# Down projection of a two-layer encoder: the seven block products in another order, one weight sum on VectorE instead of by an accumulating DMA, residual tiles in a tag of their own

## The chip, the cores and the metric

The kernel runs on one core of a Trainium2 chip. The metric is the device time of one execution in microseconds (us), given as the median over several runs. A profile is one execution of the same program, taken by the hardware profiler; its span starts with the first recorded instruction and ends with the last one.

## The reference

Two encoder layers work on a residual stream `x` of 1024 tokens by 1024 channels in float32. Each layer has an attention part (windowed in the first layer, a grid neighbourhood in the second, both with memory heads) and then a SwiGLU channel mixer. The change lies in the last matrix product of that mixer:

```
def reference(x, mem, ...):
    for i in range(DEPTH):                       # DEPTH = 2
        ...
        x = x + concat(y_tok, y_mem) @ w_out[i]
        h = rmsnorm(x, norm_ffn[i])
        gu = h @ w_gate_up[i]                    # (1024, 2 * 2816)
        x = x + (silu(gu[..., :D_FF]) * gu[..., D_FF:]) @ w_down[i]   # w_down[i]: (2816, 1024)
    return rmsnorm(x, norm_final)
```

## The kernel before, in words

**Arithmetic.** Activations lie with channels on the 128 partitions and tokens along the free side. Every float32 operand of a matmul is split into a high part (`hi`, line 106, a cast on ScalarE) and a low part (`lo`, line 109, a subtraction on VectorE). Each product is then three matmuls: high by high, high by low, low by high.

**The down projection** is done as a block product after Strassen and Winograd. The weight is cut into four blocks (even or odd 128-row blocks of the 2816 rows; first or second 512 columns), the activations into four as well, and seven products of block sums give what eight plain products would. The code numbers the products `i` = 0 to 6. The right sides (sums of activations) have been written to the DRAM tensors `b_d` by the gate-and-up stage (`hand_over`, lines 1001 to 1020). The left sides are made in place from the weight blocks by `left_side`:

- product 0 uses block `a` (even rows, first columns), which stays in SBUF in the first half of a tile `wd_kept`;
- product 1 uses the block of odd rows and first columns, loaded into a tile of the tag `raw`;
- product 3 uses `b`, the sum of the two blocks of the second columns; `b` is the second half of `wd_kept`;
- product 2 uses `b - a`, written over `a` (line 1083), so that it needs the sum that product 3 uses too;
- product 4 uses the first-column block minus the second-column block of the even rows. It is made while product 3 is prepared, over `b`, from two loads (lines 1099 to 1103);
- product 5 uses the odd first-column block minus the new `a` (line 1092), product 6 the odd second-column block.

The sum `b` is made by `first_sum` (lines 1057 to 1064): a plain load puts one block into `b`, and then a DMA that GpSimd issues on its own queue adds the other block onto it (`accum_op`, line 1062).

**Groups.** The 11 row blocks of a product are taken two at a time: `groups` has five of two and a last one of one. A full group is 24 matmuls (4 output tiles `m`, 2 row blocks, 3 terms), the last 12, a product 132. The main loop (lines 1218 to 1252) walks `dorder`, the pairs of product and group; at each step it calls `left_side` and `right_side` for the pair two places ahead. The split left sides `wd` rotate through 3 buffers (tag `whl`), the raw loads through 5 (tag `raw`), the `wd_kept` tiles are 6, and the right sides (`b_raw` from `b_d`, split into `hB`) share 16 buffers of the tag `h`.

**Results.** Products 0, 2 and 4 gather in four PSUM banks called `X`; products 1, 3 and 5 in four called `Y`; product 6 takes new `X` banks. A `start` flag clears a bank at products 0, 1, 3 and 6. After the last group of a product, `read` (lines 1144 to 1165) adds each bank on VectorE to the stream's tile `x` (line 1146). The residuals `xr` for this come back from DRAM by `residual` (lines 1121 to 1130), two tiles of the tag `raw` at a time.

**What sets the order.** The code does not fix the order in which an engine's instructions stand: a scheduler lays them out at build time, engine by engine, and may put an instruction far ahead of where the code calls it. Once laid out, each engine takes its queue strictly in order, and an instruction that waits holds up all that stand behind it. SyncE (SP) issues nearly all DMAs in the same way.

Of the kernel before, what the change touches and what calls it, by code (L numbers as in the profile page):

```python
# [9 lines left out]
F32 = mybir.dt.float32  # L10
# [7 lines left out]
P = 128  # L18
# [23 lines left out]
def trunk_kernel(ctx: ExitStack, tc: tile.TileContext, a: dict, out: bass.AP):  # L42
# [323 lines left out]
    for layer in range(2):  # L366
# [427 lines left out]
        with tc.tile_pool(name=f"fp{layer}", bufs=1, reuse_waits="tile") as fp:  # L794
# [259 lines left out]
                    kept[g] = fp.tile([P, 2, 2, HS], F32, tag="t8", name="wd_kept", bufs=6)[:, :n]  # L1054
                    rows(kept[g][:, :, 0], g, 0, slice(0, HS))

            def first_sum(g):

                p, n = groups[g]
                b, second_cols = kept[g][:, :, 1], slice(HS, D)  # L1060
                rows(b, g, 0, second_cols)
                nc.gpsimd.dma_start(
                    b, wd[p : p + n, 1].rearrange("n r c -> r n c")[:, :, second_cols], accum_op=ALU.add
                )

            def left_side(i, g):

                p, n = groups[g]
                first_cols, second_cols = slice(0, HS), slice(HS, D)

                def raw():
                    return raw_tile("wd_raw").rearrange("p (n c) -> p n c", c=HS)[:, :n]

                if i == 0:
                    keep_rows(g)
                a, b = kept[g][:, :, 0], kept[g][:, :, 1]
                if i == 0:
                    src = a
                elif i == 1:
                    src = raw()  # L1080
                    rows(src, g, 1, first_cols)
                elif i == 2:
                    nc.vector.tensor_tensor(a, b, a, op=ALU.subtract)
                    src = a
                elif i == 3:
                    src = b
                elif i == 4:
                    src = b
                elif i == 5:
                    src = raw()  # L1090
                    rows(src, g, 1, first_cols)
                    nc.vector.tensor_tensor(src, src, a, op=ALU.subtract)
                else:
                    src = raw()
                    rows(src, g, 1, second_cols)
                w = wp.tile([P, 2, D], F32R, tag="whl", name="wd", bufs=3)
                hi(two(w[:, 0], n), src)
                lo(two(w[:, 1], n), src, two(w[:, 0], n))
                if i == 3:
                    r = raw()  # L1100
                    rows(r, g, 0, first_cols)
                    rows(b, g, 0, second_cols)
                    nc.vector.tensor_tensor(b, r, b, op=ALU.subtract)
                for q in range(n):
                    left[i, p + q] = w[:, :, q * HS : (q + 1) * HS]

# [14 lines left out]
            def residual(i):  # L1121

                if i in (0, 2, 3, 4):
                    m0, f = {0: (0, 1), 2: (0, 0), 3: (4, 0), 4: (4, 1)}[i]
                    for m in range(m0, m0 + 4, 2):
                        t = raw_tile("xr").rearrange("p (n c) -> p n c", c=HS)
                        nc.sync.dma_start(
                            t, xr_d[layer][m : m + 2].rearrange("m p t -> p m t")[:, :, f * HS : (f + 1) * HS]
                        )
                        residuals[m, f], residuals[m + 1, f] = t[:, 0], t[:, 1]  # L1130
# [84 lines left out]
                if u.j == NF - 1 and n in (3, 4, 5):  # L1215
                    right_side(0, n - 3)
            norms = [Norm(), Norm() if is_a else Norm(HS, 7)]
            dorder = [(i, g) for i in range(7) for g in range(len(groups))]
            parts = iter(())
            hT = [[None] * NK, [None] * NK]  # L1220
            for at_, (i, g) in enumerate(dorder):
                if at_ + 2 < len(dorder):
                    left_side(*dorder[at_ + 2])
                    if at_ > 0:
                        right_side(*dorder[at_ + 2])
                if 1 <= at_ <= len(groups):
                    first_sum(at_ - 1)
                p, n = groups[g]
                if g == 0:
                    if i in (0, 6):  # L1230
# [115 lines left out]
```

## Time and profile before

| what | before |
|---|---|
| median of 3 runs | 2178.63 us (2178.58 to 2181.23) |
| the profiled execution | 2178.81 us |
| its span | 2176.9 us |
| busy share of the span: PE, DVE, ACT, POOL | 97%, 65%, 48%, 23% |
| mean granted TensorE clock | 0.989 |
| DMA moved | 287.22 MB, mean 132 GB/s |

PE is TensorE, DVE is VectorE, ACT is ScalarE, POOL is GpSimd. A row of a timeline gives start, duration, engine, line, operation, tiles and, in brackets, how long the engine sat idle before it and what ended that. Neighbouring instructions of the same kind are merged into one row with a count; PE's rows overlap a little, since matmuls are pipelined, so that the time of a block of matmuls is best taken from the start of one row to the start of the next. Line numbers are those of the kernel before.

### The profile page before, as it was taken

How to read it: one execution, taken by the hardware profiler on the slowest of the kernel's cores; microseconds unless marked ns; L12 is line 12 of the kernel's file. 1: busy time of each engine (PE TensorE's matmuls, PEld its weight loads, DVE VectorE, ACT ScalarE, POOL GpSimd, SP SyncE). 2: the span in 40 equal slices, each digit the busy share in tenths (PEclk: the TensorE clock that was granted, in tenths of full speed). 3: DMA queues.
4: the chain of work that ended last, by engine and by line, in shares of the span. 5: the costliest groups of instructions: out<-in, count | busy, mean ns of one | idle time of the engine just before them, and what ended most of it. 6: DMA issues, size and time to landing. Idle time of an engine off the chain costs nothing.

```text
span 2176.9 us, 28022 instructions
## 1 busy us (share of the span) xinstructions
PE 2120.3 (97%) x9946; PEld 1745.9 (80%) x9946; DVE 1408.2 (65%) x2302; ACT 1047.0 (48%) x1988; POOL 511.0 (23%) x557
## 2 busy tenths in 40 slices
PE   7999999999999999999999999999999999998997
PEld 6788888788888887788778888887888888887886
DVE  7676787775555555666766666667865455556575
ACT  6577785443333333434466566653433333343342
POOL 0344330223333321000233223203232233210000
PEclk9999999999999999999999999999999999999998
DMA  6321028333232238665232222274233232277652
GB/s 245 100 93 49 30 74 285 107 97 121 97 108 94 98 113 279 224 231 197 97 98 66 73 68 82 62 263 143 83 98 113 100 116 97 97 256 224 222 187 92
DMA packets 120076, 287.22 MB, mean 132 GB/s; under 512 B 12288, under 2 KB 18688, under 8 KB 119936
## 3 DMA queue, kind: packets, MB, share of 16 engines
q1 hardware_dynamic: 109888, 266.81, 37.0%
q10 hardware_dynamic: 7040, 12.85, 1.6%
q0 software_dynamic: 3008, 5.77, 1.5%
q8 instruction: 79, 1.29, 0.2%
q14 instruction: 61, 0.50, 0.1%
HBM read 210.40 MB, written 68.94 MB: 128 GB/s over the span
## 4 chain that ended last, share of the span: by engine, by line
PE 73%; issue 14%; DVE 4%; DMA 3%; ACT 3%; POOL 1%; SPq 0%; DVEq 0%; POOLq 0%; ACTq 0%
PE X L879 21%; PE Y L879 16%; PE mm L139 13%; PE X L1178 5%; PE Y L1178 4%; PE po L139 4%; PE S L559 3%; PE O L622 3%; PE pT L602 2%; DMA b_raw<-b_d 1%; ACT p L574 1%; DMA wd_kept<-in_w_dn 1%; DVE pl L109 1%; DMA wm_raw<-in_w_mem 1%; PE bc L242 0%
## 5 line engine op out<-in xcount | busy, mean ns | idle before, releaser
L879 PE MATMUL X<-hT,wgu 128*128 128x512 f32 x1056 | 259.1, 395 | 0.6 <-ACT g L896 0.6
L879 PE MATMUL Y<-hB,wgu 128*128 128x512 f32 x1056 | 255.5, 391 | 0.0
L1178 PE MATMUL X<-hB,wd 128*128 128x512 f32 x1056 | 246.4, 394 | 7.9 <-DVE wd L109 7.9
L879 PE MATMUL X<-hB,wgu 128*128 128x512 f32 x1056 | 247.8, 390 | 0.0
L1178 PEld LDWEIGHTS X<-hB,wd 128*128 128x128 f32 x1056 | 200.4, 190 | 51.4 <-DVE wd L109 8.7
L879 PEld LDWEIGHTS X<-hT,wgu 128*128 128x128 f32 x1056 | 198.2, 188 | 48.2 <-ACT g L896 1.0
L879 PEld LDWEIGHTS Y<-hB,wgu 128*128 128x128 f32 x1056 | 198.2, 188 | 43.4 <-issue 1.0
L879 PEld LDWEIGHTS X<-hB,wgu 128*128 128x128 f32 x1056 | 198.3, 188 | 41.8
L106 ACT CAST wgu<-wS 128x1024 fp32r<-128x1024 f32 x88 | 92.5, 1051 | 257.8 <-POOL wS L838 157.1
L587 POOL TENSOR_SCALAR p<-p,stat 128x384 f32<-128x384 f32 (+1 forms) x256 | 140.8, 569 | 313.3 <-DVE stat L584 203.7
L109 DVE TENSOR_TENSOR wgu<-wgu_raw,wgu 128x1024 fp32r<-128x1024 f32 (+1 forms) x88 | 84.8, 964 | 189.5 <-ACT wgu L106 189.5
L139 PE MATMUL mm<-hT,wqk 128*128 128x512 f32 x672 | 199.9, 405 | 0.1
L1178 PE MATMUL Y<-hB,wd 128*128 128x512 f32 x792 | 184.8, 395 | 7.1 <-DVE wd L109 7.1
L139 PE MATMUL po<-yT,wo 128*128 128x512 f32 x768 | 184.8, 394 | 0.0
L1178 PEld LDWEIGHTS Y<-hB,wd 128*128 128x128 f32 x792 | 151.3, 191 | 39.7 <-DVE wd L109 7.9
L106 ACT CAST hB<-b_raw 128x512 fp32r<-128x512 f32 x154 | 90.3, 618 | 163.9 <-DMA b_raw<-b_d 156.8
L139 PEld LDWEIGHTS po<-yT,wo 128*128 128x128 f32 x768 | 142.4, 188 | 29.6 <-issue 1.0
L838 POOL TENSOR_TENSOR wS<-wgu_raw 128x512 f32<-128x512 f32 x44 | 73.6, 1672 | 378.9 <-DVE wgu L109 378.9
L109 DVE TENSOR_TENSOR wgu<-wS,wgu 128x1024 fp32r<-128x1024 f32 x88 | 110.4, 1254 | 62.5 <-ACT wgu L106 62.5
L574 ACT ACTIVATE p<-p,stat 128x256 f32<-128x256 f32 (+1 forms) x192 | 112.3, 586 | 52.0 <-DVE stat L570 49.4
L109 DVE TENSOR_TENSOR hB<-b_raw,hB 128x512 fp32r<-128x512 f32 x154 | 100.8, 689 | 53.1 <-ACT hB L106 52.8
L109 DVE TENSOR_TENSOR pl<-pT,ph 128x384 fp32r<-128x384 f32 (+1 forms) x256 | 118.8, 494 | 21.0 <-ACT ph L106 17.9
(161 smaller groups left out, 3782.6 us busy)
## 6 DMA issues: line engine op xcount, KB each, us to landing
wgu_raw<-in_w_gu SPq DMA_DIRECT2D x92, 512.0 KB
b_raw<-b_d SPq DMA_DIRECT2D x70, 512.0 KB
b_d<-c SPq DMA_DIRECT2D x88, 256.0 KB
wd_raw<-in_w_dn SPq DMA_DIRECT2D x40, 512.0 KB
b_d<-t SPq DMA_DIRECT2D x66, 256.0 KB
wo_raw<-in_w_out SPq DMA_DIRECT2D x32, 512.0 KB
wd_kept<-in_w_dn SPq DMA_DIRECT2D x30, 512.0 KB
x<-in_x SPq DMA_DIRECT2D x32, 256.0 KB
```

The lines of the kernel that those rows point to most:

```text
L106: nc.scalar.copy(dst, src)
L109: (eng or nc.vector).tensor_tensor(dst, src, h.bitcast(F32), op=ALU.subtract)
L139: nc.tensor.matmul(ps[:, :n], l, r, start=start and i == 0 and j == 0, stop=stop and i == len(order) - 1 and j == 2,)
L559: nc.tensor.matmul(s_[:, :n], Q[self.h][:, qb * P : (qb + 1) * P], k, start=j == 0, stop=j == 1)
L574: nc.scalar.activation(p[:, :n], p[:, :n], AF.Exp, bias=m1, scale=-1.0, accum_out=s1)
L587: nc.gpsimd.tensor_scalar(p[:, :n], p[:, :n], ri[:, i : i + 1], 1.0, op0=ALU.mult, op1=ALU.mult)
L602: nc.tensor.transpose(tr[:, j * P : (j + 1) * P], p[:, j * P : (j + 1) * P], ident)
L622: nc.tensor.matmul(o[:, c0 : c0 + w * P], self.value(j), t[:, s0 : s0 + w].rearrange("p j q -> p (j q)"), start=j == js[0] and t is self.p ...
L838: sub = lambda o, p_, q_: nc.gpsimd.tensor_tensor(o, p_, q_, op=ALU.subtract)
L879: nc.tensor.matmul(ps, l, r, start=n in (0, 1, 3, 6) and k == 0 and i == 0, stop=k == 3 and i == 2, skip_group_check=True,)
L1178: nc.tensor.matmul(bank, l, r, start=i in (0, 1, 3, 6) and p == 0 and n == 0, stop=p == HF - 1 and n == 2, skip_group_check=True,)
```

## The change

The products are now walked in the order 0, 1, 3, 2, 4, 5, 6. `first_sum` and its accumulating DMAs are gone: at product 3 two raw tiles are loaded on SP's queue and added on VectorE into `b`. Product 2 still takes `b - a`, and now comes after product 3. The difference for product 4 is made at product 4 from two raw tiles. The residuals take tiles of the tag `S` (2 buffers, which the gate-and-up stage uses before) in place of tiles of the tag `raw`.

```
-            def first_sum(g):
-                p, n = groups[g]
-                b, second_cols = kept[g][:, :, 1], slice(HS, D)
-                rows(b, g, 0, second_cols)
-                nc.gpsimd.dma_start(
-                    b, wd[p : p + n, 1].rearrange("n r c -> r n c")[:, :, second_cols], accum_op=ALU.add
-                )
...
                 elif i == 3:
+                    r, o = raw(), raw()
+                    rows(r, g, 0, second_cols)
+                    rows(o, g, 1, second_cols)
+                    nc.vector.tensor_tensor(b, r, o, op=ALU.add)
                     src = b
                 elif i == 4:
-                    src = b
+                    src, o = raw(), raw()
+                    rows(src, g, 0, first_cols)
+                    rows(o, g, 0, second_cols)
+                    nc.vector.tensor_tensor(src, src, o, op=ALU.subtract)
...
-                if i == 3:
-                    r = raw()
-                    rows(r, g, 0, first_cols)
-                    rows(b, g, 0, second_cols)
-                    nc.vector.tensor_tensor(b, r, b, op=ALU.subtract)
...
-                        t = raw_tile("xr").rearrange("p (n c) -> p n c", c=HS)
+                        t = fp.tile([P, 2, HS], F32, tag="S", name="xr", bufs=2)
...
-            dorder = [(i, g) for i in range(7) for g in range(len(groups))]
+            dorder = [(i, g) for i in (0, 1, 3, 2, 4, 5, 6) for g in range(len(groups))]
...
-                if 1 <= at_ <= len(groups):
-                    first_sum(at_ - 1)
```

**Order, first place: VectorE's queue at the end of product 0 in the first layer, before.** `wd_kept_7395`, `7412`, `7440`, `7535`, `7574` and `7613` are the kept tiles of groups 0 to 5; `wd_7615` is the left side of the last group of product 0, and `wd_7655` that of the first group of product 1.

```order
L109 TENSOR_TENSOR hB_7620<-b_raw_7618,hB_7620 128x512
L1083 TENSOR_TENSOR wd_kept_7412<-wd_kept_7412 128x2x512
L1083 TENSOR_TENSOR wd_kept_7440<-wd_kept_7440 128x2x512
L109 TENSOR_TENSOR wd_7615<-wd_kept_7613,wd_7615 128x512
L109 TENSOR_TENSOR hB_7660<-b_raw_7658,hB_7660 128x512
L109 TENSOR_TENSOR hB_7663<-b_raw_7658,hB_7663 128x512
L1083 TENSOR_TENSOR wd_kept_7535<-wd_kept_7535 128x2x512
L1083 TENSOR_TENSOR wd_kept_7574<-wd_kept_7574 128x2x512
L109 TENSOR_TENSOR hB_7699<-b_raw_7697,hB_7699 128x512
L109 TENSOR_TENSOR wd_7655<-wd_raw_7653,wd_7655 128x1024
L109 TENSOR_TENSOR hB_7702<-b_raw_7697,hB_7702 128x512
L1083 TENSOR_TENSOR wd_kept_7613<-wd_kept_7613 128x512
```

The same place now (the last group of product 0 is `wd_7611`, the first of product 1 `wd_7649`):

```order
L109 TENSOR_TENSOR hB_7616<-b_raw_7614,hB_7616 128x512
L109 TENSOR_TENSOR wd_7574<-wd_kept_7572,wd_7574 128x1024
L109 TENSOR_TENSOR hB_7654<-b_raw_7652,hB_7654 128x512
L109 TENSOR_TENSOR hB_7657<-b_raw_7652,hB_7657 128x512
L109 TENSOR_TENSOR wd_7611<-wd_kept_7609,wd_7611 128x512
L109 TENSOR_TENSOR hB_7691<-b_raw_7689,hB_7691 128x512
L109 TENSOR_TENSOR hB_7694<-b_raw_7689,hB_7694 128x512
L109 TENSOR_TENSOR hB_7724<-b_raw_7722,hB_7724 128x512
L109 TENSOR_TENSOR wd_7649<-wd_raw_7647,wd_7649 128x1024
```

Before, the subtractions of line 1083, which product 2 needs a whole product later, stand among the `lo` steps of products 0 and 1; now none stands there.

**Order, second place: VectorE's queue around the end of the second product walked (product 1), before.** `wd_7879` and `wd_7915` are the left sides of the first two groups of the next product.

```order
L109 TENSOR_TENSOR wd_7846<-wd_raw_7844,wd_7846 128x512
L109 TENSOR_TENSOR hB_7952<-b_raw_7950,hB_7952 128x512
L109 TENSOR_TENSOR hB_7955<-b_raw_7950,hB_7955 128x512
L109 TENSOR_TENSOR wd_7879<-wd_kept_7395,wd_7879 128x1024
L109 TENSOR_TENSOR hB_7988<-b_raw_7986,hB_7988 128x512
L109 TENSOR_TENSOR hB_7991<-b_raw_7986,hB_7991 128x512
L1146 TENSOR_TENSOR x1_01_7710<-Y_7742,x1_01_7710 128x512
L109 TENSOR_TENSOR wd_7915<-wd_kept_7412,wd_7915 128x1024
L1146 TENSOR_TENSOR x1_11_7715<-Y_7743,x1_11_7715 128x512
```

The same place now. Lines 1080 and 1074 of the changed kernel are the sum for product 3 and the difference for product 2; line 1139 is the read of a bank (1146 before); `wd_7871` and `wd_7911` belong to the first two groups of product 3.

```order
L109 TENSOR_TENSOR wd_7834<-wd_raw_7832,wd_7834 128x512
L1080 TENSOR_TENSOR wd_kept_7440<-wd_raw_7942,wd_raw_7943 128x2x512
L1074 TENSOR_TENSOR wd_kept_7440<-wd_kept_7440 128x2x512
L109 TENSOR_TENSOR hB_7952<-b_raw_7950,hB_7952 128x512
L109 TENSOR_TENSOR hB_7955<-b_raw_7950,hB_7955 128x512
L109 TENSOR_TENSOR wd_7871<-wd_kept_7395,wd_7871 128x1024
L1080 TENSOR_TENSOR wd_kept_7535<-wd_raw_7986,wd_raw_7987 128x2x512
L1074 TENSOR_TENSOR wd_kept_7535<-wd_kept_7535 128x2x512
L109 TENSOR_TENSOR hB_7996<-b_raw_7994,hB_7996 128x512
L109 TENSOR_TENSOR hB_7999<-b_raw_7994,hB_7999 128x512
L1139 TENSOR_TENSOR x1_01_7700<-Y_7730,x1_01_7700 128x512
L109 TENSOR_TENSOR wd_7911<-wd_kept_7412,wd_7911 128x1024
```

Four sums and four differences now stand in this queue between the last read of product 0 and the first read of product 1, two of each in these rows.

**Order, third place: TensorE's queue over the whole down projection of a layer** (line 1178 before is line 1171 now).

```order
-L1178 MATMUL X<-hB,wd 128x512 x132
-L1178 MATMUL Y<-hB,wd 128x512 x132
-L1178 MATMUL X<-hB,wd 128x512 x132
-L1178 MATMUL Y<-hB,wd 128x512 x132
-L1178 MATMUL X<-hB,wd 128x512 x132
-L1178 MATMUL Y<-hB,wd 128x512 x132
-L1178 MATMUL X<-hB,wd 128x512 x48
+L1171 MATMUL X<-hB,wd 128x512 x132
+L1171 MATMUL Y<-hB,wd 128x512 x264
+L1171 MATMUL X<-hB,wd 128x512 x264
+L1171 MATMUL Y<-hB,wd 128x512 x132
+L1171 MATMUL X<-hB,wd 128x512 x48
```

The banks no longer alternate from product to product: product 3 starts in the `Y` banks right behind product 1, and product 4 goes on in the `X` banks right behind product 2.

## The prediction

> **What bounds the kernel now.** I read the page first:
>
> ```profile
> span 2176.9 us, 28022 instructions
> ...
> PE 2120.3 (97%) x9946; PEld 1745.9 (80%) x9946; DVE 1408.2 (65%) x2302; ACT 1047.0 (48%) x1988; POOL 511.0 (23%) x557
> ```
>
> TensorE is busy for 97% of the span, so only time in which it stands still, or runs slowly, can be won. The groups of the down projection are among the few with idle time in front:
>
> ```profile
> L1178 PE MATMUL X<-hB,wd 128*128 128x512 f32 x1056 | 246.4, 394 | 7.9 <-DVE wd L109 7.9
> L1178 PE MATMUL Y<-hB,wd 128*128 128x512 f32 x792 | 184.8, 395 | 7.1 <-DVE wd L109 7.1
> ```
>
> That is 15.0 us of idle, all put down to VectorE's `lo` step on a left side. Next, TensorE's timeline over both down projections, to see where it lies:
>
> ```profile
> 838.09 27.82 PE L1178 MATMUL X<-hB,wd 128*128 128x512 f32 x122
> 870.69 4.43 PE L1178 MATMUL X<-hB,wd 128*128 128x512 f32 x10 [4.79 <-DVE wd L109]
> 874.96 0.63 PE L1178 MATMUL Y<-hB,wd 128*128 128x512 f32 x2
> 878.66 31.11 PE L1178 MATMUL Y<-hB,wd 128*128 128x512 f32 x130 [3.07 <-DVE wd L109]
> 909.61 30.08 PE L1178 MATMUL X<-hB,wd 128*128 128x512 f32 x132
> 939.53 30.08 PE L1178 MATMUL Y<-hB,wd 128*128 128x512 f32 x132
> ```
> ```profile
> 1936.23 27.82 PE L1178 MATMUL X<-hB,wd 128*128 128x512 f32 x122
> 1967.16 4.07 PE L1178 MATMUL X<-hB,wd 128*128 128x512 f32 x10 [3.11 <-DVE wd L109]
> 1975.69 32.07 PE L1178 MATMUL Y<-hB,wd 128*128 128x512 f32 x130 [4.00 <-DVE wd L109]
> 2007.60 30.08 PE L1178 MATMUL X<-hB,wd 128*128 128x512 f32 x132
> ```
>
> All of it lies where product 0 ends and product 1 begins, at the same matmul in both layers: the last group of product 0, then the first of product 1. An undisturbed product takes 939.53 - 909.61 = 29.92 us, or 0.2267 us for each of its 132 matmuls and 5.44 us for a full group. Products 0 and 1 together should take 59.84 us; they take 909.61 - 838.09 = 71.52 us in the first layer and 2007.60 - 1936.23 = 71.37 us in the second. The excess is 11.68 + 11.53 = 23.21 us, more than the idle rows add up to. The stretches say why (the columns are the stretch, its length, busy time of five engines, granted clock, DMA share, GB/s):
>
> ```profile
> 850.00:860.00 10.00, 10.00 (x46) 8.29 (x45) 5.40 (x6) 2.13 (x5) 3.60 (x3) 1.00 1.06 395
> 860.00:870.00 10.00, 5.91 (x27) 4.54 (x25) 2.42 (x3) 1.24 (x3) 1.20 (x1) 0.90 1.09 275
> 870.00:880.00 10.00, 6.24 (x15) 4.69 (x16) 7.42 (x11) 4.25 (x6) 0.90 (x1) 0.67 0.61 106
> ```
>
> The granted clock falls to 0.67 behind the stall, and the ten matmuls between the two stalls take 4.27 us in place of 2.27. The Trainium skill ("TensorE: Matmul & The Clock Gate", Part 1) says that after an idle window of about 3.4 us the array runs at half clock for about 3.4 us of work. By that rule each layer, with one idle stretch beyond 3.4 us, would lose 1.7 us to the clock, an estimate from that page, and the excess would be 15.0 + 3.4 = 18.4 us; the trace shows the slower clock but 23.2 us, and the measured product times decide.
>
> Why is the `lo` late? VectorE's timeline at that place:
>
> ```profile
> 856.02 0.69 DVE L109 TENSOR_TENSOR hB<-b_raw,hB 128x512 fp32r<-128x512 f32 x1 [0.94 <-ACT hB L106]
> 864.35 1.23 DVE L1083 TENSOR_TENSOR wd_kept<-wd_kept 128x1024 f32<-128x1024 f32 x1 [7.64 <-DMA wd_kept<-in_w_dn]
> 868.81 1.23 DVE L1083 TENSOR_TENSOR wd_kept<-wd_kept 128x1024 f32<-128x1024 f32 x1 [3.23 <-DMA wd_kept<-in_w_dn]
> 869.95 0.68 DVE L109 TENSOR_TENSOR wd<-wd_kept,wd 128x512 fp32r<-128x512 f32 x1
> ...
> 872.26 1.23 DVE L1083 TENSOR_TENSOR wd_kept<-wd_kept 128x1024 f32<-128x1024 f32 x1 [0.42 <-DMA wd_kept<-in_w_dn]
> 875.65 1.23 DVE L1083 TENSOR_TENSOR wd_kept<-wd_kept 128x1024 f32<-128x1024 f32 x1 [2.16 <-DMA wd_kept<-in_w_dn]
> 876.79 0.69 DVE L109 TENSOR_TENSOR hB<-b_raw,hB 128x512 fp32r<-128x512 f32 x1
> 877.39 1.22 DVE L109 TENSOR_TENSOR wd<-wd_raw,wd 128x1024 fp32r<-128x1024 f32 x1
> ```
>
> The `lo` at 869.95, which releases TensorE, stands behind two subtractions for product 2 that wait for an accumulating DMA (7.64 + 3.23 us); the `lo` at 877.39 stands behind two more. The second product's left side is ready to be split, and queues behind work needed 30 us later. The DMAs themselves (lines 1062 and 1083 asked for by source):
>
> ```profile
> DMA to landing us min/median/max: 5.1/10.3/13.8
> ```
> ```profile
>   DMA wd_kept<-in_w_dn: 37.0, 10
> ```
>
> An accumulation lands 10.3 us after its issue, and VectorE waits 37.0 us for them over both layers. The Trainium skill ("DMA: Bandwidth & Descriptors", Anatomy of one DMA) fits such a transfer as about 2.0 us plus bytes over 436 GB/s, 3.2 us for 512 KB as an estimate from it; the trace disagrees with 10.3 us, in stretches in which the DMA engines have no free time (shares of 1.06 and 1.09 above).
>
> **The change part by part.**
>
> *Accumulations and hoisted subtractions go.* The twelve accumulating DMAs and the subtractions that waited for them leave products 0 and 1. The `lo` steps there now stand behind only their own casts and loads. If nothing else is late, both pairs of products take 59.84 us: minus 23.21 us. GpSimd's queue holds nothing else there, so nobody gains or loses by its part.
>
> *DMA traffic moves.* Each group of a layer had eight loads, one of them accumulating; it has eight plain ones now. In the window from 820 to 900 us (packets, MB, share of 16 engines):
>
> ```profile
> q1 hardware_dynamic: 8363, 19.15, 67.6%
> q0 software_dynamic: 1504, 2.88, 19.9%
> ```
>
> An accumulated MB cost 19.9/2.88 = 6.9% of 80 us, or 5.5 us, a plain one 2.8 us. The 2.88 MB accumulated and the 2.88 MB under them leave that window: 15.9 + 8.1 = 24 us of its 70 us of DMA time. What is late next there, the `b_raw` loads, gets this room. So I see no new stall in products 0 and 1.
>
> *The sums on VectorE and their waits.* Six sums per layer are new; differences are as many as before. Their prices come from the nearest operations, the difference of two loaded tiles and the `lo` of a right side:
>
> ```profile
> L1103 DVE TENSOR_TENSOR wd_kept<-wd_raw,wd_kept x12: 691/1224/1226, 937.6 to 2063.0; 128x1024 f32<-128x1024 f32 x10, 128x512 f32<-128x512 f32 x2
> ```
> ```profile
> L109 DVE TENSOR_TENSOR hB<-b_raw,hB 128x512 fp32r<-128x512 f32 x44 | 28.6, 689 | 14.4 <-ACT hB L106 14.3
> ```
>
> Twelve sums of up to 1.22 us are 14 us of work on an engine at 65%. Whether it is hidden depends on product 1, into which the new order puts four sums and four differences ahead of the first read of `Y`. From the last read of product 0 to that read, VectorE's queue holds twelve operations of 1.22 us (those eight, four full `lo`) and twelve of 0.69 us (eleven `hB`, the half `lo`): 14.6 + 8.3 = 22.9 us. For the time it has, the end of product 1 before:
>
> ```profile
> 901.65 1.05 ACT L106 CAST wd<-wd_kept 128x1024 fp32r<-128x1024 f32 x1 [0.72 <-PE Y L1178]
> ...
> 907.77 0.69 DVE L1146 TENSOR_TENSOR x<-Y,x 128x512 f32<-128x512 f32 x1 [1.02 <-PE Y L1178]
> 908.38 1.22 DVE L109 TENSOR_TENSOR wd<-wd_kept,wd 128x1024 fp32r<-128x1024 f32 x1
> 909.51 1.88 DVE L1146 TENSOR_TENSOR x<-Y,x 128x512 f32<-128x512 f32 x3
> ```
>
> A product's reads end 909.51 + 1.88 - 909.61 = 1.8 us after the next one's start, and the first can begin 1.84 us before it (909.61 - 907.77). That leaves 29.92 - 1.8 - 1.84 = 26.3 us: it fits, with 3.4 us to spare.
>
> *The bank switch.* This is a new wait: product 3 starts in the banks that product 1 has just filled, and product 4 in those of product 2. Before, a bank had a whole product to be read; now bank 0 must be read by the next product's start. By the rows above it is read at 907.77 + 0.69 = 908.46, 1.15 us early, and bank 1 at 909.51 + 0.63 = 910.14, against 909.61 + 6 x 0.2267 = 910.97, 0.83 us early. Nothing is paid as long as VectorE is not late. But in front of the read now stand a sum, a difference and two `hB` behind the `lo` of product 3's first group. That `lo` can't come sooner than its buffer, freed by the fourth group of product 1, 36 matmuls or 8.16 us before the end; a cast of 1.05 us (the first row above) and the `lo` of 1.22 us leave 5.89 us; then 2 x 1.22 + 2 x 0.69 = 3.82 us, which leaves 2.07 us, just ahead of the 1.84 us at which the read can begin. So VectorE may be 0.2 + 1.15 = 1.35 us late there before TensorE feels it. Between products 2 and 4 no sums stand in the way by the order.
>
> How late may a sum be? It waits for two raw loads; queued behind it are the `lo` steps and the reads, and TensorE behind those. The nearest row is the wait of line 1103's two loads in the first layer (us, times, longest):
>
> ```profile
> DVE wd_kept L1103 <- DMA wd_kept<-in_w_dn: 4.4, 5, 1.9
> ```
>
> Bounds: nothing if loads are early; if the whole 4.4 us falls ahead of the switch, 4.4 - 1.35 = 3.1 us per layer. Below nothing is excluded, since a wait doesn't speed TensorE. I take one wait of the longest kind per layer with half a chance: (1.9 - 1.35)/2 x 2 = about 0.6 us in all.
>
> *Loads for products 3 and 4.* Each group now needs two raw loads and a `b_raw`, 1.57 MB in 5.44 us, 289 GB/s, just ahead of use. Before, the same three per group were loaded through product 3, for use a product later:
>
> ```profile
> 940.00:950.00 10.00, 10.00 (x46) 8.29 (x45) 8.31 (x10) 2.79 (x4) 0.00 (x0) 1.00 0.93 308
> 950.00:960.00 10.00, 10.00 (x46) 8.29 (x45) 5.29 (x7) 3.75 (x6) 0.00 (x0) 1.00 0.72 259
> 960.00:970.00 10.00, 10.00 (x46) 8.29 (x45) 5.88 (x8) 4.18 (x6) 0.00 (x0) 1.00 0.80 285
> ```
>
> The engines gave 259 to 308 GB/s there with share to spare (0.72 to 0.93), and 395 when pressed (850 to 860). I cost it at nothing; the cover is the 5 raw tiles, two and a half groups.
>
> *Residuals* in tag `S`: each pair waits on SP for the reads of the pair before it, with `b_raw` and raw loads queued behind; a product's 29.92 us covers them. Nothing.
>
> **Sum.** The profiled execution takes 2178.81 us, 1.91 us more than its span and 0.18 above the median of 2178.63. 2178.63 - 23.21 + 0.6 = 2156.0 us.
>
> **Rivals.** *A, the wait comes back at the bank switch.* Waits of 4.4 us ahead of each 1-to-3 switch cost 3.1 us of idle, and some 2 us at a slow clock as behind the old stalls (4.27 - 2.27): 5 us per layer, 2155.4 + 10 = 2165.4. It decides from 1.35 us of lateness on. For it: VectorE's queue there is nearly full. Against: 3.4 us to spare over the whole product.
>
> *B, the DMA engines were the cause, not the accumulations.* At shares of 1.06 to 1.09 other loads were late too. If only the removed share of DMA time, 24 of 70, comes off the stall, the gain is 8 us: 2170.7. Against: VectorE's rows name the accumulation each time.
>
> *C, slower: the raw ring is too short for products 3 and 4.* If loads come at less than demand, each group waits. At the lowest window, 259 GB/s, a group takes 6.07 us, 3.5 us per product, 14 us over four products: 2169. The point from which it decides is 23.2/4 = 5.8 us per product, 8.65 MB in 35.7 us, 242 GB/s; at 200 GB/s a product takes 43.2 us, 53 us in all, 2155.4 + 53 = 2208 us. For it: no stock of a product's length any more. Against: the rows above.
>
> *D, no change*: new stalls that happen to come to 19 to 27 us, about 2178.
>
> **How the numbers follow.** Forecast 0.78, A 0.12, B 0.04, C 0.04, D 0.02. About 0.2% (4.4 us) is what a measurement can tell from no change. Faster: 0.78 + 0.12 + 0.04 = 0.94; same 0.02; slower 0.04. The low end is full recovery, 2155.4, less the 1.4 us by which runs may differ: 2154.0. The high end takes 3.1 us per layer from the bounds: 2155.4 + 6.2 = 2161.6, taken as 2162, part of the way to A.
>
> **What would show it.** Right: TensorE's rows without idle in all products, 59.8 us for the first two, no granted clock below 1.00 there, no software queue. Wrong: idle ahead of the first `Y` matmuls of product 3 put down to the read (A), of product 0's last group (B), or ahead of groups of products 3 and 4 with raw loads as the cause (C).

## The result, and the profile after

The changed kernel takes 2157.01 us (median of 5 runs, 2156.16 to 2159.35), the kernel before 2178.63 us (5 runs, 2177.85 to 2182.36): a ratio of 0.9897, 95% interval 0.9883 to 0.9912; the medians are 21.6 us apart. The forecast was 2156.0 us. The profiled execution's span is 2155.1 us where it was 2176.9 us, 21.8 us less, and the mean granted clock went from 0.989 to 0.993.

TensorE's timeline over both down projections, the rows that answer to those of before (start, length, what, how many, idle ahead in brackets):

```profile
837.38 30.08 PE L1171 MATMUL X<-hB,wd 128*128 128x512 f32 x132
867.30 60.00 PE L1171 MATMUL Y<-hB,wd 128*128 128x512 f32 x264
927.14 60.00 PE L1171 MATMUL X<-hB,wd 128*128 128x512 f32 x264
...
1925.67 30.08 PE L1171 MATMUL X<-hB,wd 128*128 128x512 f32 x132
1955.59 60.00 PE L1171 MATMUL Y<-hB,wd 128*128 128x512 f32 x264
2015.43 60.00 PE L1171 MATMUL X<-hB,wd 128*128 128x512 f32 x264
```

No row has a bracket. The first three products take 927.14 - 837.38 = 89.76 us and 2015.43 - 1925.67 = 89.76 us, exactly three times 29.92: the 23.21 us of the old stall are gone, and nothing has come in their place at the bank switch. The page's groups and its queues of data transfers say the same:

```profile
q1 hardware_dynamic: 112896, 272.57, 37.8%
q10 hardware_dynamic: 7040, 12.85, 1.6%
...
L879 PE MATMUL Y<-hB,wgu 128*128 128x512 f32 x1056 | 256.8, 392 | 1.6 <-ACT c L899 1.6
...
L1171 PE MATMUL X<-hB,wd 128*128 128x512 f32 x1056 | 242.1, 390 | 0.0
...
L1171 PE MATMUL Y<-hB,wd 128*128 128x512 f32 x792 | 180.2, 389 | 0.0
```

The idle of 7.9 and 7.1 us is 0.0, and there is no software queue any more. The largest new wait is 1.6 us ahead of a gate-and-up pass (L879), behind ScalarE's line 899. The kernel before waits at that stage behind line 896, for 0.6 us:

```profile
L879 PE MATMUL X<-hT,wgu 128*128 128x512 f32 x1056 | 259.1, 395 | 0.6 <-ACT g L896 0.6
```

At this stage TensorE so waits 1.0 us longer than before. Between the stall removed and the span gained lie 23.2 - 21.8 = 1.4 us; since other rows of TensorE's waits moved too, from 0.8 us less to 0.6 us more, the 1.4 us are not settled by this stage alone.

VectorE at the end of product 1, where the new sums (L1080) and the read of the bank (L1139) stand:

```profile
881.98 1.23 DVE L1080 TENSOR_TENSOR wd_kept<-wd_raw 128x1024 f32<-128x1024 f32 x1 [1.29 <-DMA wd_raw<-in_w_dn]
...
886.77 1.23 DVE L1080 TENSOR_TENSOR wd_kept<-wd_raw 128x1024 f32<-128x1024 f32 x1 [0.49 <-DMA wd_raw<-in_w_dn]
...
891.53 1.22 DVE L1080 TENSOR_TENSOR wd_kept<-wd_raw 128x1024 f32<-128x1024 f32 x1
892.78 1.23 DVE L1074 TENSOR_TENSOR wd_kept<-wd_kept 128x1024 f32<-128x1024 f32 x1
893.92 1.29 DVE L109 TENSOR_TENSOR hB<-b_raw,hB 128x512 fp32r<-128x512 f32 x2
895.38 0.69 DVE L1139 TENSOR_TENSOR x<-Y,x 128x512 f32<-128x512 f32 x1 [0.17 <-PE Y L1171]
```

Two sums did wait for their raw loads, 1.78 us together, and the last sum, difference and two `hB` stand right ahead of the read. But when VectorE reached the read it still had to wait 0.17 us for TensorE: it was not late (second layer: 1.92 us of waits for raw loads, 0.15 us for TensorE). The prediction had put this at 0.2 us. The stretches (length, busy time of five engines, clock, DMA share, GB/s) show how full the place is:

```profile
870.00:880.00 10.00, 10.00 (x46) 8.26 (x45) 7.44 (x10) 3.86 (x5) 0.00 (x0) 1.00 0.99 335
880.00:890.00 10.00, 10.00 (x46) 8.29 (x45) 8.14 (x10) 3.50 (x6) 0.00 (x0) 1.00 0.98 364
890.00:900.00 10.00, 10.00 (x46) 8.28 (x45) 9.80 (x12) 4.74 (x7) 0.00 (x0) 1.00 0.80 305
```

VectorE is busy for 9.80 of the 10 us around the switch, and in the 20 us before them the DMA engines have a share of 0.98 to 0.99. It fits, with little to spare.

### The profile page after: what moved, and what is told of

Read it like the earlier page. It is cut to its first block, busy times and chain, and to the rows that moved or that the text cites. A ratio compares the mean times of both kernels' runs of the same rounds, so it can differ in the third digit from the quotient of the medians.

```text
span 2155.1 us, 28039 instructions
## 1 busy us (share of the span) xinstructions
PE 2113.1 (98%) x9946; PEld 1740.9 (81%) x9946; DVE 1417.9 (66%) x2314; ACT 1045.6 (49%) x1988; POOL 498.2 (23%) x545
## 4 chain that ended last, share of the span: by engine, by line
PE 43%; issue 4%; DVE 2%; ACT 2%; POOL 1%; DMA 0%; DVEq 0%; SPq 0%; POOLq 0%; ACTq 0%
PE X L879 11%; PE mm L139 9%; PE Y L879 8%; PE X L1171 5%; PE Y L1171 4%; PE po L139 2%; PE S L559 2%; PE O L622 1%; PE pT L602 1%; ACT p L574 0%; DMA b_raw<-b_d 0%; PE bc L242 0%; DVE pl L109 0%; DVE wqk L109 0%; PE vtr L419 0%
## 5 line engine op out<-in xcount | busy, mean ns | idle before, releaser
L879 PE MATMUL X<-hT,wgu 128*128 128x512 f32 x1056 | 259.1, 395 | 0.0
L879 PE MATMUL Y<-hB,wgu 128*128 128x512 f32 x1056 | 256.8, 392 | 1.6 <-ACT c L899 1.6
L879 PE MATMUL X<-hB,wgu 128*128 128x512 f32 x1056 | 247.8, 390 | 0.0
L879 PEld LDWEIGHTS X<-hT,wgu 128*128 128x128 f32 x1056 | 198.2, 188 | 47.3
L879 PEld LDWEIGHTS Y<-hB,wgu 128*128 128x128 f32 x1056 | 198.5, 188 | 46.3 <-ACT c L899 2.5
L879 PEld LDWEIGHTS X<-hB,wgu 128*128 128x128 f32 x1056 | 198.3, 188 | 41.7
L1171 PE MATMUL Y<-hB,wd 128*128 128x512 f32 x792 | 180.2, 389 | 0.0
L233 POOL TENSOR_TENSOR nr<-nv,neg_half 128x4 f32<-128x4 f32 (+1 forms) x11 | 11.7, 1063 | 587.0 <-DVE nv L232 586.8
L106 ACT CAST wgu<-wgu_raw 128x1024 fp32r<-128x1024 f32 (+1 forms) x88 | 73.4, 835 | 122.5 <-PE Y L879 73.7
```

Source lines behind the costliest of these rows:

```text
L106: nc.scalar.copy(dst, src)
L233: nc.gpsimd.tensor_tensor(r[:, :nb], v[:, :nb], neg_half[:, :nb], op=ALU.pow)
L879: nc.tensor.matmul(ps, l, r, start=n in (0, 1, 3, 6) and k == 0 and i == 0, stop=k == 3 and i == 2, skip_group_check=True,)
L1171: nc.tensor.matmul(bank, l, r, start=i in (0, 1, 3, 6) and p == 0 and n == 0, stop=p == HF - 1 and n == 2, skip_group_check=True,)
```

## The experiments

Two questions were open. Which part of the change earns the gain? And was the old stall due to where the subtractions stood in VectorE's queue (the theory of the prediction), or to the load that the accumulating DMAs put on the DMA engines (its rival B)? Below, "products 0+1" is the time from the start of product 0 to the start of product 2: 59.84 us undisturbed, 71.52 and 71.37 us before. The diffs are against the kernel before, those of sum_only and of the three kernels whose names begin with "after" against the changed kernel.

### The parts alone

**sum_only**: the changed kernel's sums and residual tiles, with the old order of products; the sum is made at product 2, just ahead of the difference that needs it.

```diff
-                    nc.vector.tensor_tensor(a, b, a, op=ALU.subtract)
-                    src = a
-                elif i == 3:
...
                     nc.vector.tensor_tensor(b, r, o, op=ALU.add)
+                    nc.vector.tensor_tensor(a, b, a, op=ALU.subtract)
+                    src = a
+                elif i == 3:
...
-            dorder = [(i, g) for i in (0, 1, 3, 2, 4, 5, 6) for g in range(len(groups))]
+            dorder = [(i, g) for i in range(7) for g in range(len(groups))]
```

> Product order 0 to 6 as before; the sum comes from two raw tiles added on VectorE while product 2 is prepared, so there is no accumulating DMA; residuals in their own tag as in the change. Queue theory (the loss came from subtractions that stood in VectorE's queue at the end of product 0 and waited for accumulating DMAs): those waits are gone, products 0 and 1 take 59.8 us together in both layers, time 2155 to 2159 us. Order theory (the new product order gives the gain): the stall stays, 71.4 us for the two products, about 2178 us.

Measured: 2159.23 us, ratio 0.9901 (0.9877 to 0.9924). In TensorE's timeline of the first layer, product 0 and product 2 start 899.00 - 839.16 = 59.84 us apart:

```profile
839.16 30.08 PE L1171 MATMUL X<-hB,wd 128*128 128x512 f32 x132
...
899.00 30.08 PE L1171 MATMUL X<-hB,wd 128*128 128x512 f32 x132
```

The whole gain is there without the new order: the interval overlaps the changed kernel's.

**order_only**: the kernel before, with products 3 and 2 exchanged and the difference made at product 2.

```diff
-                if i == 3:
+                if i == 2:
...
-            dorder = [(i, g) for i in range(7) for g in range(len(groups))]
+            dorder = [(i, g) for i in (0, 1, 3, 2, 4, 5, 6) for g in range(len(groups))]
```

> Only the product order is changed to 0, 1, 3, 2, 4, 5, 6; the accumulating DMAs and the residual tiles are as before, and the difference for product 4 is made while product 2 is prepared. Queue theory: the scheduler still puts the subtractions for product 2 at the end of product 0, behind the same DMAs, so products 0 and 1 take about 71.4 us and the time is 2176 to 2182 us. Order theory: 59.8 us and 2155 to 2159 us.

Measured: 2180.50 us, ratio 0.9997 (0.9986 to 1.0009). The old stall stands where it stood:

```profile
869.55 3.97 PE L1178 MATMUL X<-hB,wd 128*128 128x512 f32 x10 [2.80 <-DVE wd L109]
...
878.14 61.86 PE L1178 MATMUL Y<-hB,wd 128*128 128x512 f32 x262 [4.16 <-DVE wd L109]
```

The first three products take 100.90 us (838.94 to 939.84), 11.14 us more than 89.76. The order by itself shows neither a cost nor a gain.

**residual_only**: the kernel before, with the residual pairs in tiles of their own.

```diff
-                        t = raw_tile("xr").rearrange("p (n c) -> p n c", c=HS)
+                        t = fp.tile([P, 2, HS], F32, tag="S", name="xr", bufs=2)
```

> The kernel before with the residuals in tiles of tag S and nothing else. Queue theory: the accumulating DMAs and the waiting subtractions stay, so does the loss; in VectorE's queue one of the two subtractions ahead of product 0's last left side now stands behind it and three stand ahead of product 1's first, so the stall moves from the end of product 0 to the first group of product 1; the two products together take 69 to 73 us, time 2174 to 2182 us. Residual theory (raw tiles held by residuals bring the loads of product 1 late): 59.8 us, 2155 to 2159 us.

Measured: 2183.39 us, ratio 1.0008 (0.9997 to 1.0020). The stall changes its shape, not its size:

```profile
866.90 2.58 PE L1178 MATMUL X<-hB,wd 128*128 128x512 f32 x10 [0.42 <-DVE wd L109]
...
878.41 31.42 PE L1178 MATMUL Y<-hB,wd 128*128 128x512 f32 x130 [6.76 <-DVE wd L109]
```

What product 0's last group no longer waits, product 1 waits more; products 0+1 take 71.02 us (838.66 to 909.68). This run also has the new wait of the changed kernel behind ScalarE's line 899, 1.4 us in all.

### The cause of the old stall

**pool_sub**: the kernel before, its subtractions of line 1083 on GpSimd, which has little else to do there.

```diff
-                    nc.vector.tensor_tensor(a, b, a, op=ALU.subtract)
+                    nc.gpsimd.tensor_tensor(a, b, a, op=ALU.subtract)
```

> The kernel before with one word changed: the subtraction for product 2 (line 1083) runs on GpSimd in place of VectorE. The accumulating DMAs, their bytes and the product order stay. Queue theory: VectorE no longer waits for them, products 0 and 1 take 59.8 us, 2155 to 2159 us; GpSimd needs about 3.3 us for each (twice the 1.67 us of its 128x512 operations) and has until product 2 starts, 60 us later. Rival B (the DMA engines, filled by the accumulations, bring the other loads late): the engines are as full as before, so most of the stall stays: 2170 to 2179 us.

Measured: 2168.07 us, ratio 0.9945 (0.9925 to 0.9964). Products 0+1 take 66.46 and 66.76 us: 13.5 of the 23.2 us stay. Neither theory alone had forecast that: the time is below the 2170 to 2179 us of rival B and above the 2155 to 2159 us of the other. What now comes last is ScalarE (first row) and then VectorE:

```profile
868.11 0.73 PE L1178 MATMUL Y<-hB,wd 128*128 128x512 f32 x2 [1.46 <-ACT wd L106]
870.99 7.27 PE L1178 MATMUL Y<-hB,wd 128*128 128x512 f32 x24 [2.15 <-DVE wd L109]
```

The run also brings in something that was not there before. VectorE's `lo` beside a subtraction of GpSimd:

```profile
848.73 3.46 DVE L109 TENSOR_TENSOR wd<-wd_kept,wd 128x1024 fp32r<-128x1024 f32 x1 [1.49 <-ACT wd L106]
```
```profile
848.72 2.38 POOL L1083 TENSOR_TENSOR wd_kept<-wd_kept 128x1024 f32<-128x1024 f32 x1 [6.98 <-issue]
```

The `lo` takes 3.46 us in place of 1.22. The Trainium skill ("SBUF — State Buffer", SBUF: two separate sides) says that a VectorE operation with two SBUF inputs and a GpSimd operation that reads SBUF exclude one another for a whole instruction. That gives 2.38 + 1.22 = 3.60 us, and the trace agrees. GpSimd's own queue changes as well: the accumulations, which it issues, now stand behind the subtractions, and the last of the first layer is issued at 877.66 where it was 871.74. So this run does not separate the two causes cleanly; the next two do.

**late_sub**: the kernel before, with its accumulating DMAs as they are, but one operand of each subtraction multiplied by a 1 that exists only once product 0's bank has been read. It can't be placed among the `lo` steps of the end of product 0.

```diff
-                    nc.vector.tensor_tensor(a, b, a, op=ALU.subtract)
+                    nc.vector.scalar_tensor_tensor(
+                        a, b, late[0], a, op0=ALU.mult, op1=ALU.subtract
+                    )
...
+                    if m == 0:
+                        late.append(sp.tile([P, 1], F32, tag="late", name="late", bufs=2))
+                        nc.vector.tensor_scalar(late[0], x[0][1][:, :1], 0.0, 1.0, op0=ALU.mult, op1=ALU.add)
```

> The kernel before with the accumulating DMAs, the product order and the engine of every operation kept, but the subtraction for product 2 (line 1083) multiplies by a one that is worked out from the first tile read at the end of product 0, so that it cannot stand earlier in VectorE's queue than that. Queue theory alone: the loss was the subtractions' place in the queue, products 0 and 1 take 59.8 to 61 us, 2155 to 2160 us; what GpSimd's subtractions left over (66.5 us) was GpSimd and VectorE slowing each other (an lo of 3.46 us in place of 1.22). Two-cause theory: accumulations also fill the DMA engines so that right sides (b_raw) land late and hold up ScalarE's casts (8.03 us wait there): 64 to 68 us, 2164 to 2171 us.

Measured: 2165.87 us, ratio 0.9938 (0.9922 to 0.9953). Products 0+1 take 64.19 and 62.37 us: 4.35 + 2.53 = 6.9 us stay. In the first layer:

```profile
837.38 30.08 PE L1183 MATMUL X<-hB,wd 128*128 128x512 f32 x132
869.36 0.73 PE L1183 MATMUL Y<-hB,wd 128*128 128x512 f32 x2 [1.90 <-ACT wd L106]
870.62 31.11 PE L1183 MATMUL Y<-hB,wd 128*128 128x512 f32 x130 [0.53 <-DVE wd L109]
```

Product 0 is undisturbed, its last group included. Ahead of product 1 TensorE is idle for 1.90 us, until ScalarE's cast releases it. ScalarE's timeline of this run tells why:

```profile
867.75 0.62 ACT L106 CAST hB<-b_raw 128x512 fp32r<-128x512 f32 x1 [8.69 <-DMA b_raw<-b_d]
868.27 1.04 ACT L106 CAST wd<-wd_raw 128x1024 fp32r<-128x1024 f32 x1
```

The cast of the left side stands in ScalarE's queue behind one of a right side, which waited 8.69 us for a late `b_raw` load. SP did not hold that load back: it had issued it at 852.70, 15.0 us before the cast could start. And that wait was in the kernel before all along:

```profile
869.13 0.62 ACT L106 CAST hB<-b_raw 128x512 fp32r<-128x512 f32 x1 [8.76 <-DMA b_raw<-b_d]
869.66 1.04 ACT L106 CAST wd<-wd_raw 128x1024 fp32r<-128x1024 f32 x1
```

It cost nothing visible, because VectorE's `lo` came later still (877.39). Even with VectorE free the left side could not have been split before 869.66 + 1.04 = 870.70, behind an undisturbed start of product 1 at 838.09 + 29.92 = 868.01.

**no_accum_op**: the kernel before, its accumulating DMAs as plain copies, so that the addition is left out: same queue, bytes and waits.

```diff
-                    b, wd[p : p + n, 1].rearrange("n r c -> r n c")[:, :, second_cols], accum_op=ALU.add
+                    b, wd[p : p + n, 1].rearrange("n r c -> r n c")[:, :, second_cols]
```

> The kernel before without accum_op: GpSimd's DMA copies the second block over the first in place of adding it (this leaves out the addition of the sum), on the same queue, after the same wait, with the same bytes; the subtractions stay at the end of product 0. If the engine time of an accumulation matters (5.5 us per MB against 2.8 us), the transfers land in about half the time, VectorE's 18 us of waits in the first layer become 6 to 10, products 0 and 1 take 62 to 66 us, 2161 to 2171 us. If only the place in the queue and the waits behind the plain loads matter, little changes: 69 to 72 us, 2174 to 2181 us.

Measured: 2167.19 us, ratio 0.9949 (0.9932 to 0.9965). The queues from 838 to 879 us (packets, MB, share of 16 engines), of the kernel before and then of this one:

```profile
q1 hardware_dynamic: 3513, 7.65, 51.9%
q0 software_dynamic: 1504, 2.88, 38.8%
```
```profile
q1 hardware_dynamic: 4331, 9.71, 64.2%
q0 software_dynamic: 800, 2.88, 18.6%
```

Without the addition the same 2.88 MB take half the engine time. The subtractions stand where they stood and still wait, but not for so long:

```profile
837.44 30.08 PE L1178 MATMUL X<-hB,wd 128*128 128x512 f32 x132
...
870.34 31.39 PE L1178 MATMUL Y<-hB,wd 128*128 128x512 f32 x130 [2.36 <-DVE wd L109]
```
```profile
858.96 1.23 DVE L1083 TENSOR_TENSOR wd_kept<-wd_kept 128x1024 f32<-128x1024 f32 x1 [4.68 <-DMA wd_kept<-in_w_dn]
862.19 1.23 DVE L1083 TENSOR_TENSOR wd_kept<-wd_kept 128x1024 f32<-128x1024 f32 x1 [2.00 <-DMA wd_kept<-in_w_dn]
```

4.68 + 2.00 us where it was 7.64 + 3.23. ScalarE gets its `b_raw` earlier too, 13.3 us after SP issued the load at 851.62 in place of 15.0 us after 854.10:

```profile
864.89 0.62 ACT L106 CAST hB<-b_raw 128x512 fp32r<-128x512 f32 x1 [6.55 <-DMA b_raw<-b_d]
865.41 1.04 ACT L106 CAST wd<-wd_raw 128x1024 fp32r<-128x1024 f32 x1
```

Its cast of the left side ends at 866.45, ahead of product 1's start at 837.44 + 29.92 = 867.36, so here only VectorE's queue holds TensorE. Products 0+1 take 64.12 and 61.98 us: 6.4 us stay.

The two runs belong together. In the profiled executions, taking away the queue place alone wins 16.3 of 23.2 us, and relieving the DMA engines alone wins 16.8: together more than the whole. The two profiled executions, though, took 2161.99 and 2162.26 us, 4 to 5 us less than the medians of their four runs. By the medians the gains are 13.0 and 11.6 us, 24.6 in sum, against 21.6 for the changed kernel, and the intervals of the ratios leave room for a sum of no more than that. What stands firm is that each half alone brings a large part of the gain, and that neither brings it all: both intervals lie above that of the changed kernel. That the two overlap is read from the rows: ScalarE's wait and VectorE's wait run side by side, and removing one uncovers the other. The stall is a late transfer seen through an in-order queue. Only with both gone (sum_only and the changed kernel) is it 0.

**late_acc**: the kernel before, with loads, accumulations and subtractions held back until product 0's bank has been read (`late[0]` is made as in late_sub).

```diff
+                nc.vector.tensor_copy(b[:, 0, :1], late[0])
...
-                if 1 <= at_ <= len(groups):
-                    first_sum(at_ - 1)
+                if 6 <= at_ < 6 + len(groups):
+                    first_sum(at_ - 6)
```

> The kernel before with the plain load and the accumulation of each sum held back until the first tile is read at the end of product 0 (a one-column write into the block that depends on it stands ahead of them). The subtractions for product 2 then stand among the lo steps at the end of product 1, again behind the accumulations. Two-cause theory: the loss leaves products 0 and 1's border and follows the accumulations: product 0 takes 29.9 us, products 1 and 2 together 66 to 76 us in place of 59.8, 2165 to 2185 us. If the loss belongs to the place (the end of gate and up and its b_d traffic, beside which any two more transfers are too many), it stays small when they are moved: products 0 to 2 under 92 us, 2157 to 2162 us.

Measured: 2182.87 us in one run, beside 2177.75 for the kernel before on that chip. TensorE's timeline in the first layer:

```profile
842.21 30.08 PE L1182 MATMUL X<-hB,wd 128*128 128x512 f32 x132
872.13 27.84 PE L1182 MATMUL Y<-hB,wd 128*128 128x512 f32 x122
902.94 3.94 PE L1182 MATMUL Y<-hB,wd 128*128 128x512 f32 x10 [2.98 <-DVE wd L109]
...
912.46 31.50 PE L1182 MATMUL X<-hB,wd 128*128 128x512 f32 x130 [5.12 <-DVE wd L109]
943.79 30.08 PE L1182 MATMUL Y<-hB,wd 128*128 128x512 f32 x132
```

Product 0 is undisturbed now, and the stall is at the end of product 1, of the old size: 943.79 - 872.13 = 71.66 us for products 1 and 2, and 71.78 in the second layer. VectorE's subtractions (line 1084 here) wait there as they did a product earlier:

```profile
891.78 1.22 DVE L1084 TENSOR_TENSOR wd_kept<-wd_kept 128x1024 f32<-128x1024 f32 x1 [11.36 <-DMA wd_kept<-in_w_dn]
```

The stall goes with the accumulations and their subtractions, not with anything at the start of the projection. The 5 us by which this run is longer than the kernel before do not lie in the projection's stall; most of them are there when the first projection starts (at 842.21, and at 838.09 in the profile of before), and they were not traced.

### How much room the new place has

These three add to the changed kernel, to see which limit of the new form comes first. Each is one run, beside 2179.99 us of the kernel before on that chip.

**after_sum2** makes each sum twice, **after_sum6** six times:

```diff
                     nc.vector.tensor_tensor(b, r, o, op=ALU.add)
+                    nc.vector.tensor_tensor(b, r, o, op=ALU.add)
```

> The changed kernel with every sum for product 3 made twice (the same result written again): six more VectorE operations of 1.22 us per layer, four of them ahead of the first read of Y if the order stays. By the prediction's account VectorE has 3.4 us to spare in product 1 and 1.15 us more before TensorE feels a late read, 4.5 us together; four more sums take 4.9 us. So the switch from product 1 to 3 stalls by 0.4 us per layer at most, less if the scheduler moves differences behind the reads; first two products 59.8 us, first three 89.8 to 90.2 us, time within 1 us of the changed kernel. If VectorE was already the limit there (rival A nearer than thought): 4 to 5 us per layer, about 2166 us.

> The changed kernel with every sum for product 3 made six times: 5.5 x 5 x 1.22 = 33.6 us more VectorE work per layer, in products 1 and 3. The left side of a group of product 3 then costs VectorE 6 x 1.22 + 1.22 (lo) + 1.38 (two hB) = 9.9 us against 5.44 us of TensorE's. VectorE can hide 3.4 us in product 1 and less than 12 us (40% of 29.9) in product 3, so products 1 and 3 together lose 10 to 25 us per layer, behind the switch above all in the groups of product 3; time 2175 to 2205 us. If VectorE is not near its limit there, as a busy share of 66% of the span would have it, the loss is under 5 us per layer.

Measured: 2160.25 and 2184.55 us. The first product after the bank switch, in after_sum2 and then in after_sum6:

```profile
899.73 30.52 PE L1172 MATMUL Y<-hB,wd 128*128 128x512 f32 x132 [0.86 <-DVE x L1140]
```
```profile
903.45 11.12 PE L1176 MATMUL Y<-hB,wd 128*128 128x512 f32 x48 [1.12 <-DVE x L1144]
...
932.06 11.13 PE L1176 MATMUL Y<-hB,wd 128*128 128x512 f32 x36 [4.73 <-ACT wd L106]
```

With four more sums ahead of the switch, 4 x 1.22 = 4.9 us, the first three products take 91.22 and 90.99 us, 1.46 and 1.23 us over 89.76. The expectation was 0.4 us at most, from 3.4 + 1.15 us of room, so the room was smaller than that; the time, 2160.25 us in one run, is 3.2 above the changed kernel's median where 1 was expected at most. The 3.4 us count VectorE's work alone. In the first layer of after_sum2 VectorE also stood idle between the reads of the two products, for 2.2 us until a raw load landed and for 1.9 us until ScalarE's casts were done, and these waits come out of the same room. With six sums the loss is 10.95 and 10.71 us per layer, within the 10 to 25 that were expected, and most of it has moved on from the switch into product 3's own groups.

**after_traffic** stores each sum to memory twice, through GpSimd's queue:

```diff
+                    for d in (layer, 1 - layer):
+                        dst = y_d[d][g][:, : n * HS].rearrange("r (n c) -> r n c", c=HS)
+                        nc.gpsimd.dma_start(dst, b)
```

> The changed kernel with two stores of each sum (512 KB each) to unused DRAM from GpSimd's queue: 1.05 MB more per group of product 3, besides the 1.57 MB of its loads, 482 GB/s if it had to keep pace with 5.44 us per group; the most seen in a stretch was 395. If DMA bandwidth is close behind (rival C), product 3's groups slow to 2.62 MB / 395 = 6.6 us, 6.5 us per layer and more with slow clocks: 2168 to 2180 us. If the 5 raw tiles and the time to product 3 cover it, under 2 us per layer: up to 2161 us.

Measured: 2168.23 us. TensorE and VectorE in the first layer:

```profile
901.25 30.52 PE L1174 MATMUL Y<-hB,wd 128*128 128x512 f32 x132 [2.39 <-DVE x L1142]
```
```profile
884.74 1.23 DVE L1080 TENSOR_TENSOR wd_kept<-wd_raw 128x1024 f32<-128x1024 f32 x1 [2.58 <-DMA wd_raw<-in_w_dn]
...
896.19 1.23 DVE L1080 TENSOR_TENSOR wd_kept<-wd_raw 128x1024 f32<-128x1024 f32 x1 [1.46 <-DMA wd_raw<-in_w_dn]
```

The raw loads come later, the sums wait 2.58 + 0.39 + 1.46 = 4.43 us, and the loss (2.98 and 5.97 us) appears at the bank switch, put down to the read. Product 3's groups, which take their raw tiles just ahead of use, run on without idle. The time lies in the range that the expectation gave to rival C, but the place of the loss is that of rival A. So under this load the form breaks as rival A described. The two layers break at waits of 4.43 and 6.01 us; the changed kernel, with 1.78 and 1.92, does not, and where between 1.92 and 4.43 us it starts was not measured.

## Why the prediction was right, and where it was not

- **The accumulations and hoisted subtractions go, -23.21 us.** Right, to the hundredth: products 0+1 take 59.84 us in both layers, and sum_only shows that this part alone does it.
- **The order, the residuals, the loads of products 3 and 4, at nothing.** Right within what was measured: order and residuals alone have 0.9997 and 1.0008, both intervals across 1, and there is no idle ahead of any group of products 3 and 4. The residuals were not quite free, as the last point says. The cover for the loads was thinner than the prediction read it, a share of 0.98 to 0.99 at the end of product 1 where it had quoted 0.72 to 0.93.
- **The bank switch, +0.6 us.** It measured 0. The step's arithmetic held (0.17 us of wait for TensorE against 0.2 worked out), and the sums' waits, 1.78 and 1.92 us, were absorbed by the room ahead of it. The 3.4 us of room beyond that were too many (after_sum2).
- **DMA relief costs and gains nothing further.** Too small a part. Rival B was set aside because VectorE's rows name the accumulation each time. The runs show that the load on the DMA engines is a part of the mechanism of its own: no_accum_op wins by it alone, 16.8 us in the profiled execution and 11.6 by the medians, and with the queue place gone, 6.9 us stay in the profile of late_sub. The row that said so is ScalarE's wait of 8.76 us for `b_raw`, in the trace of before; it was hidden by the later wait, and the prediction did not quote it. So its sentence that product 1's left side is ready to be split holds only from 870.70 on, when ScalarE's cast ends, and not at the 868.01 at which an undisturbed product 1 would have started. The total is untouched, because the change removes queue place and load at once. Rival B's sum, a gain of 8 us from the removed share of DMA time, was wrong as well: no_accum_op, which takes only part of that time away, won more than 8 us.
- **The sum.** 2156.0 forecast, 2157.01 measured. By spans, 1.4 us of the 23.21 are missing. The largest new row is the wait in gate and up behind line 899, 1.0 us more than before; the prediction gave no term to that stage, whose lines the change does not touch. The runs show which part of the change brings it: the row stands in all six kernels whose residuals take tiles of the tag `S` (1.1 to 2.1 us; residual_only, which changes nothing else, 1.4) and in none of the six others, which wait for at most 1.0 us behind line 896. In the changed kernel line 899's copy stands in ScalarE's queue behind a cast that waits 4.14 us for a `b_raw` load. The rest of the 1.4 us was not traced. That the forecast came within about 1 us owes something to luck: the 0.6 us put down for the bank switch did not come, and partly made up for the wait that had no term.

No run pointed to a version beyond the changed kernel: its down projection has no idle left ahead of its matmuls.

## What to carry to other kernels

When a wait of an in-order engine disappears, look at what the other engine on the same input was doing at that time: a wait that ends earlier is not in the idle rows of the bound engine, though it is the next to bind. To find whether a late transfer or the queue behind it is at fault, move the one and shorten the other in two separate runs. If the two gains add to more than the whole by more than the spread of the runs, they are parts of one chain; here the spread was too wide for the sum to say so, and the rows had to. And an accumulating DMA is to be weighed by its DMA engine time, which was twice that of a copy here, and not by its bytes alone, against an addition on an engine with room.

## What was not expected of the hardware

- An accumulating DMA took twice the DMA engine time of a copy of the same bytes on the same queue: 38.8% against 18.6% of 16 engines over 41 us, for 2.88 MB.
- A VectorE operation that met a GpSimd subtraction took 3.46 us in place of 1.22, so moving work to an idle GpSimd was not free for VectorE.
- Short idle times of TensorE cost clock in some places and not in others. Undisturbed, 130 matmuls take 30.08 - 2 x 0.2267 = 29.63 us. In the first layers of no_accum_op and late_sub, behind 2.36 us and 1.90 + 0.53 us of idle, they took 31.39 and 31.11 us, and the granted clock was 0.50 from 872 to 874 us in the one and 0.54 from 870 to 872 us in the other. In the second layers of the same two kernels, behind 1.85 and 1.26 + 0.53 us, they took 29.76 and 29.94 us, at a clock of 1.00. That looks like a limit at about 2 us of idle, but after_traffic speaks against it: behind 2.39 us its clock stayed at 1.00 (900 to 910 us), and its 132 matmuls took 30.52 us in place of 30.08. So the length of one idle time does not decide alone; what else does stays open.
